# Where the norm weight goes: into the tokens' parts instead of every weight unit, low parts of weights on GpSimd, and the residual read back from memory

## The chip, the cores and the metric

The kernel runs on one core of one Trainium2 chip. The metric is the time of one execution on the device, in microseconds (us). TensorE (PE) multiplies matrices, PEld is its weight load; VectorE is DVE, ScalarE is ACT, GpSimd is POOL; SyncE (SP) issues most of the transfers between memory and the core's buffers.

## The reference

One inference step of two layers on 1032 tokens (1024 of a prompt, 8 decode tokens), 1024 features, float32. What matters here is where a norm stands ahead of a projection, and the residual:

```python
def rms_norm(x, w):
    y = x32 * lax.rsqrt(jnp.mean(x32 * x32, axis=-1, keepdims=True) + NORM_EPS)
    return (y * w.astype(jnp.float32)).astype(x.dtype)
...
    for layer in range(DEPTH):
        h = rms_norm(x, norm_mix[layer])
        ...                                   # layer 0: hybrid mixer, layer 1: SSD mixer; both begin with h @ w_in
        x = x + out                           # and end with @ w_out
        x = x + squared_relu_mlp(rms_norm(x, norm_mlp[layer]), mlp_w1[layer], mlp_w2[layer])
    return (rms_norm(x, norm_final), ...)
```

Layer 0 (gated delta rule and retention) projects 1024 features to 28 tiles of 128, layer 1 (SSD) to 40 and 32 columns more; each MLP goes to 4096 features and back.

## The kernel before

All activations lie with features on the partitions: a tile is 128 features by 1032 tokens. The residual stream x is held as two exact parts, `xh[k]` (rounded to float32r) and `xl[k]` (the rest), 8 tiles each. A weight is split in the same way, and a product is three matmuls (`mm3`, lines 150 to 152): high by high, high by low, low by high, each 128 x 128 by 344 tokens.

`load_w` (line 132) brings a weight unit [128, 512]: a transfer by SyncE into `raw` (3 buffers), then for a projection behind a norm GpSimd scales `raw` by the norm weights of its features (line 140), ScalarE copies it to the high part `whi` (line 144), and VectorE takes the low part `wlo` (line 145). The units of the second projections (`w_out`, `w2`), which have no norm weight, leave line 140 out and take their low part on GpSimd. The pairs of parts have 6 buffers, thus three units. The norm's other factor, the reciprocal root `rstd_bc`, scales the products when they leave the accumulators.

Stages, in order: the head (`load_x`: tokens arrive, `xh`, `xl`, their squares, the first tile's products); the hybrid mixers, where pieces of the projections are emitted between pieces of the mixers' chunk recurrences; near their end `out_first` (line 466), the first 3 (layer 1: 4) k-tiles of the output projection for all 8 m-tiles in three pieces of 344 tokens, to which the residual is added, before the sum goes to memory (`accd`); `out_proj` (line 1328), which loads these sums into `acc`, adds the remaining k-tiles and splits the new residual (`split_piece`, line 225); the MLP (`up`: a hidden tile, squared and split; `down`: a block of four hidden tiles onto `acc`); the same for layer 1 with the SSD mixer (`ssd_group`, line 1569). In `ssd_group` VectorE makes `xdt` (line 1600) and the masked scores `sc` (line 1613), and TensorE's decay products (line 1621) follow them.

In `out_first` the sum of a piece is built in `ost`: VectorE adds the product and `xh` (line 473), GpSimd adds `xl` (line 474), SyncE stores it (line 475). In layer 0 pieces 0 and 1 of an m-tile share a buffer of which there are two ("cs"), piece 2 has one buffer ("rb"); in layer 1 an m-tile's three pieces share one of four buffers.

Each engine works its instructions off in a fixed order. That order isn't the text's: a scheduler sets it when the program is built, so the change moves instructions beyond the edited lines. Each instruction waits for the semaphores of those it depends on.

Of the kernel before, what the change touches and what calls it, by code (L numbers as in the profile page):

```python
# [19 lines left out]
T = 1032                     # 1024 prompt tokens, then 8 decode tokens  # L20
# [24 lines left out]
# order of the hybrid projection's m-tiles (first column of each)  # L45
# [14 lines left out]
# blocks of the output projections: the first packed column's k-tile, the mixer outputs  # L60
# [13 lines left out]
# columns of the retention's constants  # L74
# [9 lines left out]
class Pools:  # L84
    """A mixer's two pools: what the output projection's first block needs or reuses, and the rest."""
# [10 lines left out]
class Kern:  # L96
    def __init__(self, ctx, tc, I, O):
# [20 lines left out]
        self.xl = [self.xp.tile([P, T], F32R, name=f"xl{k}") for k in range(KT)]  # L118

# [12 lines left out]
    def load_w(self, src, n, normw=None, lo_eng=None, dst=None, norm_eng=None):  # L132
        """src [128, n] of a packed weight unit -> exact float32r high and low parts."""
        nc = self.nc
        raw = self.wp.tile([P, 512], F32, tag="raw", name="raw", bufs=3)
        nc.sync.dma_start(raw[:, :n], src)
        if normw is not None:
            k = normw.shape[1]
            r3 = raw[:, :n].rearrange("p (k c) -> p k c", k=k)
            (norm_eng or nc.gpsimd).tensor_tensor(out=r3, in0=r3, in1=normw.unsqueeze(2).to_broadcast([P, k, n // k]), op=ALU.mult)  # L140
# [3 lines left out]
        nc.scalar.copy(hi[:, :n], raw[:, :n])  # L144
        (lo_eng or nc.vector).tensor_tensor(out=lo[:, :n], in0=raw[:, :n], in1=hi[:, :n].bitcast(F32), op=ALU.subtract)  # L145
        return hi, lo
# [7 lines left out]
    def load_half(self, src, kh, M, normw):  # L154
        return self.load_w(src[:, kh * 4 * M:(kh + 1) * 4 * M], 4 * M, normw[:, kh * 4:kh * 4 + 4])
# [9 lines left out]
    def products(self, src, M, normw, pss):  # L165
        """The products of an m-tile over the model dimension; yields after every sixth."""
        for kh in range(2):
            hi, lo = self.ahead.pop(0) if self.ahead else self.load_half(src, kh, M, normw)
# [12 lines left out]
    def gemm_units(self, src, M, normw, evict, other=False):  # L181
# [11 lines left out]
        for u, n in enumerate(self.products(src, M, normw, pss)):  # L193
# [31 lines left out]
    def split_piece(self, m, n, src, ssq, tp):  # L225
        """src [128, 344] fp32 becomes the residual's piece (m, n); its squares go to ssq."""
        nc = self.nc
        s = NSL[n]
        nc.scalar.copy(self.xh[m][:, s], src)  # L229
        nc.vector.tensor_tensor(out=self.xl[m][:, s], in0=src, in1=self.xh[m][:, s].bitcast(F32), op=ALU.subtract)  # L230
        self.square_piece(m, n, src, ssq, tp)
# [11 lines left out]
    def rsqrt(self, out, src):  # L243
        """out = (src) ** -0.5 for a small tile."""
# [7 lines left out]
    def rstd_from(self):  # L252
        """rstd_bc[:, t] = (sum_p ssq[p, t] / 1024 + eps) ** -0.5 on every partition; ssq lies where rstd_bc does."""
# [42 lines left out]
    def load_x(self, gp):  # L296
        """The tokens, as exact parts; their rstd; and the narrow projection, not yet scaled by it."""
# [15 lines left out]
        w0 = [self.load_half(I["wih"][0], 0, 128, normw)]  # L313
# [9 lines left out]
        def square(m):  # L323
            """x[m]'s squares; those of four tiles are added up."""
# [19 lines left out]
        for m in range(KT):  # L344
            nc.scalar.copy(self.xh[m], xr[m])
            nc.vector.tensor_tensor(out=self.xl[m], in0=xr[m], in1=self.xh[m].bitcast(F32), op=ALU.subtract)
# [4 lines left out]
            if m == 1:  # L351
                w0.append(self.load_half(I["wih"][0], 1, 128, normw))
# [21 lines left out]
    def softplus(self, out, x, tp, tag, bufs=None):  # L374
        """log1p(exp(x)) = max(x, 0) + 2 atanh(u / (2 + u)), u = exp(-|x|)."""
# [40 lines left out]
    def silu2(self, x, scale, tp):  # L416
        """x (1 + tanh(scale x)) in place, in two halves."""
# [6 lines left out]
    def layer(self, l):  # L424
        tc = self.tc
        nk = 16 if l else 8
        with ExitStack() as es:
            dp = es.enter_context(tc.tile_pool(name=f"spill{l}", bufs=1, space=bass.MemoryType.DRAM))
# [5 lines left out]
            with ExitStack() as es_op:  # L434
# [11 lines left out]
                self.out_proj(name, blocks, acc, tp, parts)  # L446
# [10 lines left out]
    def load_mixed(self, k, raw, hi, lo):  # L457
        """A spilled mixer output [128, 1024] and its decode columns, as exact parts."""
# [7 lines left out]
    def out_first(self, name, c0, parts, stage):  # L466
        """The first k-tiles of an output projection, with the residual, go to memory."""
        nc = self.nc

        def ev(m, n, ps):  # L470
            s = NSL[n]
            r = stage(n)
            nc.vector.tensor_tensor(out=r, in0=ps, in1=self.xh[m][:, s].bitcast(F32), op=ALU.add)
            nc.gpsimd.tensor_tensor(out=r, in0=r, in1=self.xl[m][:, s].bitcast(F32), op=ALU.add)
# [5 lines left out]
    def hyb_mixers(self, gp):  # L480
# [5 lines left out]
        def proj(dst, off=0):  # L486
            normw = self.V("mix0", 0, 8)
# [3 lines left out]
            yield from self.gemm_units(I["wih"][next(wi)], 128, normw, ev)  # L491
# [23 lines left out]
        def ret(t, rr, vv, gg):  # L515
            for i in range(2):
# [3 lines left out]
                for q in range(4):          # the halves of each head's features change places  # L520
# [25 lines left out]
        def step():  # L546
            """Emits a sixth of a projection (and the end of the one before)."""
# [6 lines left out]
        def project(n):  # L554
            """Emits the projections up to tile n."""
# [6 lines left out]
        def weave(mix, need, rate):  # L562
            """Emits a mixer's pieces with `rate` sixths of a projection after each."""
# [16 lines left out]
        # the output projection's first block fills in while the last mixers finish  # L580
# [22 lines left out]
    def gdn_setup(self, gp, ba):  # L603
# [14 lines left out]
        gnh = gp.tile([P, 5], F32, name="gnh")     # norm weights of the gated outputs, halved  # L618
# [4 lines left out]
        # beta and decay: [8, T] -> token-major [128, 9, 8]  # L623
# [35 lines left out]
        # rows of the cumulated decay, as exact float32r parts stacked on the contraction  # L659
# [19 lines left out]
    def gdn_head(self, gp, h, feat, st):  # L679
# [21 lines left out]
        for bi in range(2):  # L701
# [33 lines left out]
            # decay, transposed: DT[j, c, i] = exp(min(G_i - G_j, mask))  # L735
# [1150 lines left out]
```

## Time and profile before

| | |
|---|---|
| time, median of 3 runs | 3255.57 us |
| lowest and highest run | 3240.14 and 3257.78 us |
| profiled execution: first to last instruction | 3239.5 us |
| busy: TensorE, VectorE, ScalarE, GpSimd | 3086.4, 1740.3, 896.2, 1241.3 us |
| granted TensorE clock, mean | 0.960 |
| scaling of weight units (line 140) | 264 units, 300.7 us of GpSimd |
| low parts on VectorE (line 145) | 264 units, 209.6 us |
| low parts on GpSimd (line 145) | 179 units, 223.7 us |

The profile gives its span alone for the profiled execution, 3239.5 us; of the three runs the lowest, 3240.14 us, is 0.6 us longer than this span, and what lies around a span is not told otherwise. Rows read "line engine operation out<-in, shapes, xcount | busy us, mean ns of one | idle time of the engine before them, and what ended most of it". Rows of waits read "who <- whom: us in total, times, longest". A matmul's busy time overlaps its neighbours', so busy is not the same as at full rate; the granted clock says at which share of its full clock TensorE was let run.

### The profile page before, as it was taken

What the parts mean: (1) busy time and instruction counts of PE and PEld (TensorE: products, weight loads), DVE (VectorE), ACT (ScalarE), POOL (GpSimd) and SP (SyncE); (2) the same over time, 40 slices, a digit from 0 to 9 for tenths busy, and PEclk for the clock granted to TensorE, in tenths of its full rate; (3) what the DMA queues carried; (4) which work ended last, traced back from release to release, by engine and by line L of the source; (5) the groups of instructions that cost most, each with busy time, mean ns of one, the idle gap of its engine ahead of it and who ended that gap; (6) DMA issues with size and microseconds to landing.
All of it is one profiled execution on the core that took longest, in us unless ns stands there. A gap on an engine that the chain in (4) does not pass through costs nothing. (4 is left out here: it accounts for less than half of the span.)

```text
span 3239.5 us, 49390 instructions
## 1 busy us (share of the span) xinstructions
PE 3086.4 (95%) x19566; PEld 2929.6 (90%) x19566; DVE 1740.3 (54%) x3201; ACT 896.2 (28%) x1828; POOL 1241.3 (38%) x1234
## 2 busy tenths in 40 slices
PE   7989998989999999999999999999899999999998
PEld 6888888879999999999987788887899999999998
DVE  7664667464333333337886785967635333333334
ACT  3222221223111111114444444354213111111112
POOL 4232324155333323225355555444625332332324
PEclk9899999889999999999998898998899999999999
DMA  3011103142111111111111111222431111111112
GB/s 123 20 47 54 47 26 112 55 168 64 46 46 47 49 46 46 48 48 40 55 56 58 69 62 43 82 69 79 157 140 43 46 47 49 46 46 50 46 46 72
DMA packets 102326, 202.13 MB, mean 62 GB/s; under 512 B 12624, under 2 KB 27728, under 8 KB 102096
## 3 DMA queue, kind: packets, MB, share of 16 engines
q1 hardware_dynamic: 94800, 173.82, 16.7%
q0 software_dynamic: 7296, 25.17, 2.0%
q8 instruction: 154, 2.52, 0.3%
q14 instruction: 76, 0.62, 0.1%
HBM read 157.94 MB, written 38.89 MB: 61 GB/s over the span
## 5 line engine op out<-in xcount | busy, mean ns | idle before, releaser
L150 PE MATMUL pg<-xh,whi 128*128 128x344 f32 x3072 | 1020.7, 332 | 10.2 <-DVE sxc L1451 6.5
L152 PE MATMUL pg<-xh,wlo 128*128 128x344 f32 x3072 | 1012.9, 330 | 2.8 <-DVE wlo L145 2.8
L151 PE MATMUL pg<-xl,whi 128*128 128x344 f32 x3072 | 1009.0, 328 | 0.0
L150 PEld LDWEIGHTS pg<-xh,whi 128*128 128x128 f32 x3072 | 593.0, 193 | 27.7 <-issue 8.8
L152 PEld LDWEIGHTS pg<-xh,wlo 128*128 128x128 f32 x3072 | 592.8, 193 | 12.7 <-issue 5.2
L144 ACT CAST whi<-raw 128x512 fp32r<-128x512 f32 (+2 forms) x443 | 271.0, 612 | 1191.5 <-PE pg L151 723.9
L151 PEld LDWEIGHTS pg<-xl,whi 128*128 128x128 f32 x3072 | 592.3, 193 | 8.8 <-issue 5.8
L140 POOL TENSOR_TENSOR raw<-raw,vec 128x512 f32<-128x512 f32 x264 | 300.7, 1139 | 589.9 <-DMA raw<-w 339.7
L151 PE MATMUL pg<-alo,whi 128*128 128x344 f32 (+2 forms) x1476 | 472.4, 320 | 0.0
L152 PE MATMUL pg<-ahi,wlo 128*128 128x344 f32 (+2 forms) x1476 | 472.3, 320 | 0.0
L150 PE MATMUL pg<-ahi,whi 128*128 128x344 f32 (+2 forms) x1476 | 471.6, 319 | 0.0
L1236 DVE TENSOR_TENSOR acc<-acc,pg 128x344 f32<-128x344 f32 x360 | 182.8, 511 | 385.4 <-PE pg L152 385.4
L145 POOL TENSOR_TENSOR wlo<-raw,whi 128x512 fp32r<-128x512 f32 (+2 forms) x179 | 223.7, 1251 | 327.7 <-ACT whi L144 326.6
L145 DVE TENSOR_TENSOR wlo<-raw,whi 128x512 fp32r<-128x512 f32 x264 | 209.6, 794 | 193.3 <-ACT whi L144 172.2
L1227 POOL TENSOR_TENSOR r<-r 128x344 f32<-128x344 f32 x192 | 145.9, 760 | 387.6 <-ACT ahi L1226 338.5
L152 PEld LDWEIGHTS pg<-ahi,wlo 128*128 128x128 f32 x1476 | 277.6, 188 | 0.0
L150 PEld LDWEIGHTS pg<-ahi,whi 128*128 128x128 f32 x1476 | 277.5, 188 | 0.0
L151 PEld LDWEIGHTS pg<-alo,whi 128*128 128x128 f32 x1476 | 277.3, 188 | 0.0
L1228 DVE TENSOR_TENSOR alo<-r,ahi 128x344 fp32r<-128x344 f32 x192 | 135.6, 707 | 253.8 <-POOL r L1227 253.8
L1226 ACT ACTIVATE ahi<-r 128x344 fp32r<-128x344 f32 x192 | 94.5, 492 | 338.5 <-DVE r L1225 338.5
L1225 DVE SCALAR_TENSOR_TENSOR r<-pg,rstd_bc 128x344 f32<-128x344 f32 x186 | 94.8, 510 | 76.9 <-PE pg L152 75.6
L150 PE MATMUL pg<-mhi,whi 128*128 128x344 f32 x408 | 131.3, 322 | 4.1 <-DVE acc L1342 4.1
(534 smaller groups left out, 4422.9 us busy)
## 6 DMA issues: line engine op xcount, KB each, us to landing
raw<-w SPq DMA_DIRECT2D x256, 256.0 KB, 2.6
raw<-wis SPq DMA_DIRECT2D x80, 256.0 KB, 2.6
raw<-wih SPq DMA_DIRECT2D x56, 256.0 KB, 2.6
mraw<-spill SPq DMA_DIRECT2D x17, 512.0 KB, 4.1
accd<-ost SPq DMA_DIRECT2D x48, 172.0 KB, 2.1
acc<-accd SPq DMA_DIRECT2D x16, 516.0 KB, 6.9
dS<-sstate SPq DMA_DIRECT2D x32, 256.0 KB, 3.5
o_sssm<-dS POOLq DMA_DIRECT2D x32, 256.0 KB, 2.4
```

What stands on the lines that cost most here:

```text
L140: (norm_eng or nc.gpsimd).tensor_tensor(out=r3, in0=r3, in1=normw.unsqueeze(2).to_broadcast([P, k, n // k]), op=ALU.mult)
L144: nc.scalar.copy(hi[:, :n], raw[:, :n])
L145: (lo_eng or nc.vector).tensor_tensor(out=lo[:, :n], in0=raw[:, :n], in1=hi[:, :n].bitcast(F32), op=ALU.subtract)
L150: t.matmul(ps, lhsT=whi, rhs=xhi, start=start, stop=False)
L151: t.matmul(ps, lhsT=whi, rhs=xlo, start=False, stop=False)
L152: t.matmul(ps, lhsT=wlo, rhs=xhi, start=False, stop=stop)
L1225: nc.vector.scalar_tensor_tensor(out=r, in0=ps, scalar=0.0, in1=self.rstd_bc[:, s], op0=ALU.max, op1=ALU.mult)
L1226: nc.scalar.activation(hi[:, s], r, AF.Square)
L1227: nc.gpsimd.tensor_tensor(out=r, in0=r, in1=r, op=ALU.mult)
L1228: nc.vector.tensor_tensor(out=lo[:, s], in0=r, in1=hi[:, s].bitcast(F32), op=ALU.subtract)
L1236: nc.vector.tensor_tensor(out=s, in0=s, in1=ps, op=ALU.add)
```

## The change

1. Norm weights: `load_w` no longer scales. Where the residual is split, both parts carry the norm weights of the norm that follows: ScalarE's copy becomes a copy with a scale for each partition, VectorE's subtraction becomes (x * w) - high. The sums of squares still take the unscaled x. The narrow projection of the head, which reads the tokens themselves, keeps its scaled weights.
2. Low parts: all of them are now taken on GpSimd.
3. Residual: as the parts no longer hold x itself, `out_first` loads each piece of x from memory into `ost` and adds the product on top. In layer 0 it comes from the input, in layer 1 from `resd`, which the last block of layer 0's MLP fills by transfers that GpSimd issues.

```diff
     def __init__(self, ctx, tc, I, O):
...
+        rp = ctx.enter_context(tc.tile_pool(name="resd", bufs=1, space=bass.MemoryType.DRAM))
+        self.resd = [rp.tile([P, T], F32, name=f"resd_{m}") for m in range(KT)]
...
-    def load_w(self, src, n, normw=None, lo_eng=None, dst=None, norm_eng=None):
+    def load_w(self, src, n, lo_eng=None, dst=None):
         raw = self.wp.tile([P, 512], F32, tag="raw", name="raw", bufs=3)
         nc.sync.dma_start(raw[:, :n], src)
-        if normw is not None:
-            k = normw.shape[1]
-            r3 = raw[:, :n].rearrange("p (k c) -> p k c", k=k)
-            (norm_eng or nc.gpsimd).tensor_tensor(out=r3, in0=r3, in1=normw.unsqueeze(2).to_broadcast([P, k, n // k]), op=ALU.mult)
...
         nc.scalar.copy(hi[:, :n], raw[:, :n])
-        (lo_eng or nc.vector).tensor_tensor(out=lo[:, :n], in0=raw[:, :n], in1=hi[:, :n].bitcast(F32), op=ALU.subtract)
+        (lo_eng or nc.gpsimd).tensor_tensor(out=lo[:, :n], in0=raw[:, :n], in1=hi[:, :n].bitcast(F32), op=ALU.subtract)
...
-    def split_piece(self, m, n, src, ssq, tp):
-        s = NSL[n]
-        nc.scalar.copy(self.xh[m][:, s], src)
-        nc.vector.tensor_tensor(out=self.xl[m][:, s], in0=src, in1=self.xh[m][:, s].bitcast(F32), op=ALU.subtract)
+    def split(self, m, s, src, w):
+        nc.scalar.activation(self.xh[m][:, s], src, AF.Copy, scale=w)
+        nc.vector.scalar_tensor_tensor(out=self.xl[m][:, s], in0=src, scalar=w, in1=self.xh[m][:, s].bitcast(F32), op0=ALU.mult, op1=ALU.subtract)
+
+    def split_piece(self, m, n, src, ssq, tp, norm):
+        self.split(m, NSL[n], src, self.V(norm, m))
         self.square_piece(m, n, src, ssq, tp)
...
     def load_x(self, gp):
-            nc.scalar.copy(self.xh[m], xr[m])
-            nc.vector.tensor_tensor(out=self.xl[m], in0=xr[m], in1=self.xh[m].bitcast(F32), op=ALU.subtract)
+            self.split(m, slice(0, T), xr[m], self.V("mix0", m))
...
     def layer(self, l):
+            if l == 0:
+                self.resid = lambda m: self.I["xT"][:, m, :]
+            else:
+                self.resid = lambda m: self.resd[m]
...
     def out_first(self, name, c0, parts, stage):
             r = stage(n)
-            nc.vector.tensor_tensor(out=r, in0=ps, in1=self.xh[m][:, s].bitcast(F32), op=ALU.add)
-            nc.gpsimd.tensor_tensor(out=r, in0=r, in1=self.xl[m][:, s].bitcast(F32), op=ALU.add)
+            nc.sync.dma_start(r, self.resid(m)[:, s])
+            nc.vector.tensor_tensor(out=r, in0=r, in1=ps, op=ALU.add)
             nc.sync.dma_start(self.accd[m][:, s], r)
...
     def down(b):                              # in mlp
                     if b == HID // 4 - 1:
-                        self.split_piece(m, n, s, ssq, tp)
+                        self.split_piece(m, n, s, ssq, tp, "mix1")
+                        if n == 2:
+                            nc.gpsimd.dma_start(self.resd[m], acc[m])
...
     def ssm_setup(self, gp):
-                nc.gpsimd.tensor_tensor(out=raw, in0=raw, in1=normw[:, k:k + 4].unsqueeze(2).to_broadcast([P, 4, 32]), op=ALU.mult)
```

The rest of the diff hands the norm's name on to `split_piece` and takes the argument `normw` out of the calls. The counts of instructions by engine: TensorE the same, VectorE 264 fewer, GpSimd 42 fewer (266 scalings and 48 additions out, 264 low parts and 8 issues in), SyncE 48 more.

What stands where. On VectorE, in the third step of the first group of the SSM mixers (`sxc` is a projection leaving the accumulators, `x` the convolution, `dS` and `dy` the decode states), before:

```order
L421 SCALAR_TENSOR_TENSOR x<-th,x 128x516
L1727 SCALAR_TENSOR_TENSOR dS<-dbc,dxd,dS 128x128 x3
L421 SCALAR_TENSOR_TENSOR x<-th,x 128x516
L1451 TENSOR_TENSOR sxc<-pg,rstd_bc 128x344
L145 TENSOR_TENSOR wlo<-raw,whi 128x512
L1731 TENSOR_REDUCE dy<-dpr 128x4
L1451 TENSOR_TENSOR sxc<-pg,rstd_bc 128x344 x2
L1600 TENSOR_TENSOR xdt<-pm,dt 128x512
```

and now, in the same place (line numbers behind the edits have moved by one or two):

```order
L1726 SCALAR_TENSOR_TENSOR dS<-dbc,dxd,dS 128x128 x3
L421 SCALAR_TENSOR_TENSOR x<-th,x 128x516
L1450 TENSOR_TENSOR sxc<-pg,rstd_bc 128x344
L421 SCALAR_TENSOR_TENSOR x<-th,x 128x516
L1730 TENSOR_REDUCE dy<-dpr 128x4
L1450 TENSOR_TENSOR sxc<-pg,rstd_bc 128x344 x2
L1599 TENSOR_TENSOR xdt<-pm,dt 128x512
```

The low part has gone from between the two `sxc`, and half of a convolution's gate (L421) stands there instead.

On SyncE, at the end of layer 0's first block (`accd` the stored sums, `woh` weights, `mraw` a mixer's output for the next block), before:

```order
L475 DMA accd_6_103<-ost 128x344
L475 DMA accd_7_104<-ost 128x344 x2
L136 DMA raw<-woh 128x256
L475 DMA accd_7_104<-ost 128x344
L1335 DMA acc_0_6973<-accd_0_97 128x1032
```

and now:

```order
L479 DMA accd_6_113<-ost 128x344
L479 DMA accd_7_114<-ost 128x344
L477 DMA ost<-xT 128x344
L479 DMA accd_7_114<-ost 128x344
L138 DMA raw<-woh 128x256
L479 DMA accd_6_113<-ost 128x344
L477 DMA ost<-xT 128x344
L479 DMA accd_7_114<-ost 128x344
L138 DMA raw<-woh 128x384
L1338 DMA acc_0_6927<-accd_0_107 128x1032
```

The loads of the residual stand between the stores, each ahead of the store of the piece that it begins, and weights and the reload of `acc` stand behind them.

More of the change, by code (lines that the diff above doesn't have):

```diff
@@ L152, in mm3, with load_half @@
         t.matmul(ps, lhsT=wlo, rhs=xhi, start=False, stop=stop)
-    def load_half(self, src, kh, M, normw):
-        return self.load_w(src[:, kh * 4 * M:(kh + 1) * 4 * M], 4 * M, normw[:, kh * 4:kh * 4 + 4])
+    def load_half(self, src, kh, M):
+        return self.load_w(src[:, kh * 4 * M:(kh + 1) * 4 * M], 4 * M)
     def narrow(self, ps, w, x, k):
@@ L163, in narrow, with products @@
             self.nc.tensor.matmul(ps[32 * n:32 * n + M, 0:c.stop - c.start], lhsT=w, rhs=x[:, c], start=k == 0, stop=k == KT - 1)
-    def products(self, src, M, normw, pss):
+    def products(self, src, M, pss):
         for kh in range(2):
-            hi, lo = self.ahead.pop(0) if self.ahead else self.load_half(src, kh, M, normw)
+            hi, lo = self.ahead.pop(0) if self.ahead else self.load_half(src, kh, M)
             for n in range(3):
@@ L179, in others, with gemm_units @@
         return [self.pm(), self.ps2(), self.ps2()]
-    def gemm_units(self, src, M, normw, evict, other=False):
+    def gemm_units(self, src, M, evict, other=False):
         if self.first:
@@ L192, in gemm_units @@
         pss = self.others() if other else [self.pg() for n in range(3)]
-        for u, n in enumerate(self.products(src, M, normw, pss)):
+        for u, n in enumerate(self.products(src, M, pss)):
             if u == 0:
@@ L214, in gemm_flush @@
                 k1 = min(kn, k0 + cut)
-                hi, lo = self.load_w(src(m)[:, k0 * 128:k1 * 128], (k1 - k0) * 128, None, self.nc.gpsimd)
+                hi, lo = self.load_w(src(m)[:, k0 * 128:k1 * 128], (k1 - k0) * 128)
                 w += [(hi[:, i:i + 128], lo[:, i:i + 128]) for i in range(0, (k1 - k0) * 128, 128)]
@@ L312, in load_x @@
         fetch(1)
-        w0 = [self.load_half(I["wih"][0], 0, 128, normw)]
+        w0 = [self.load_half(I["wih"][0], 0, 128)]
         nc.vector.tensor_scalar(out=self.ones_r, in0=self.ident, scalar1=0.0, scalar2=1.0, op0=ALU.mult, op1=ALU.add)
@@ L351, in load_x @@
             if m == 1:
-                w0.append(self.load_half(I["wih"][0], 1, 128, normw))
+                w0.append(self.load_half(I["wih"][0], 1, 128))
             if m > 1:
@@ L445, in layer @@
                 acc = [ap.tile([P, T], F32, name=f"acc{l}_{m}") for m in range(KT)]
-                self.out_proj(name, blocks, acc, tp, parts)
+                self.out_proj(name, blocks, acc, tp, parts, "mlp%d" % l)
             self.mlp(l, acc, l == 1)
@@ L486, in proj @@
         def proj(dst, off=0):
-            normw = self.V("mix0", 0, 8)
             def ev(n, ps):
                 nc.vector.tensor_tensor(out=dst[:, off + n * NW:off + (n + 1) * NW], in0=ps, in1=self.rstd_bc[:, NSL[n]], op=ALU.mult)
-            yield from self.gemm_units(I["wih"][next(wi)], 128, normw, ev)
+            yield from self.gemm_units(I["wih"][next(wi)], 128, ev)
         def gate(k, zs):
@@ L1228, in ev @@
                     nc.vector.tensor_tensor(out=lo[:, s], in0=r, in1=hi[:, s].bitcast(F32), op=ALU.subtract)
-                self.gemm_tile(I["w1"][l, t], 128, normw, ev, t == 1)
+                self.gemm_tile(I["w1"][l, t], 128, ev, t == 1)
             def down(b):
@@ L1249, in finish @@
                         dst = (w[:, 0:512], w[:, 512:1024])
-                    ws.append(self.load_w(I["w2"][l, b, m], 512, None, nc.gpsimd, dst))
+                    ws.append(self.load_w(I["w2"][l, b, m], 512, nc.gpsimd, dst))
                 def norm(s0, s1, sqs):
@@ L1325, in mlp, with out_proj @@
                 self.rstd = self.rstd_from()
-    def out_proj(self, name, blocks, acc, tp, parts):
+    def out_proj(self, name, blocks, acc, tp, parts, norm):
         nc, tc = self.nc, self.tc
@@ L1343, in ev @@
                     if last:
-                        self.split_piece(m, n, o, ssq, tp)
+                        self.split_piece(m, n, o, ssq, tp, norm)
                 for _ in self.gemm_flush(lambda m: self.I[name][m, :, c0 * 128:c0 * 128 + w], cur, ev):
@@ L1380, in ssm_setup @@
         self.first = self.others()
-        for u, _ in enumerate(self.products(I["wis"][4], 128, normw, self.first)):
+        for u, _ in enumerate(self.products(I["wis"][4], 128, self.first)):
             if u == 1:
@@ L1443, in ssm_mixers @@
         st = self.ssm_setup(gp)
-        normw = self.V("mix1", 0, 8)
         def conv_tile(dst, ti, gst, gco):
@@ L1451, in ev @@
                 nc.vector.tensor_tensor(out=xc[:, 3 + n * NW:3 + (n + 1) * NW], in0=ps, in1=self.rstd_bc[:, NSL[n]], op=ALU.mult)
-            self.gemm_tile(I["wis"][ti // 4 * 10 + ti % 4 if ti < 16 else ti % 4 * 10 + ti // 4], 128, normw, ev)
+            self.gemm_tile(I["wis"][ti // 4 * 10 + ti % 4 if ti < 16 else ti % 4 * 10 + ti // 4], 128, ev)
             nc.gpsimd.tensor_scalar(out=gco, in0=xc[:, 3 + 1021:3 + 1032], scalar1=1.0, scalar2=None, op0=ALU.mult)
@@ L1476, in ev @@
                 nc.vector.scalar_tensor_tensor(out=z[:, NSL[n]], in0=ps, scalar=0.5, in1=self.rstd_bc[:, NSL[n]], op0=ALU.mult, op1=ALU.mult)
-            self.gemm_tile(I["wis"][g * 10 + 6 + i], 128, normw, ev)
+            self.gemm_tile(I["wis"][g * 10 + 6 + i], 128, ev)
             self.silu2(z, 1.0, gp)
```

2 lines of the change are left out of this document (removed).

## The prediction

> **What bounds the kernel now.** I read the busy line and the clock line of the page first, then the stages cut out of the span, then who ended TensorE's waits in the stages where it waits at all.
>
> ```profile
> PE 3086.4 (95%) x19566; PEld 2929.6 (90%) x19566; DVE 1740.3 (54%) x3201; ACT 896.2 (28%) x1828; POOL 1241.3 (38%) x1234
> ```
>
> By stage (columns: stretch, its length, each engine's busy time with its instructions, granted clock, DMA share, GB/s):
>
> ```profile
> core 0: us, PE busy (x) PEld busy (x) DVE busy (x) ACT busy (x) POOL busy (x), PEclk, DMA share, GB/s
> 0.00:82.00 82.00, 63.59 (x369) 51.90 (x370) 64.35 (x105) 30.55 (x51) 35.73 (x37) 0.92 0.37 121
> 82.00:648.00 566.00, 521.66 (x3672) 473.15 (x3671) 353.49 (x856) 139.36 (x292) 169.48 (x212) 0.94 0.16 52
> 648.00:718.00 70.00, 62.34 (x340) 53.09 (x340) 43.87 (x89) 12.94 (x21) 40.33 (x41) 0.87 0.40 140
> 810.00:1455.00 645.00, 645.00 (x4102) 645.00 (x4101) 222.44 (x398) 113.30 (x201) 197.77 (x199) 1.00 0.15 47
> ...
> 1530.00:2260.00 730.00, 683.03 (x4099) 605.74 (x4098) 560.39 (x887) 330.88 (x755) 350.58 (x313) 0.92 0.18 62
> 2260.00:2350.00 90.00, 76.49 (x434) 73.09 (x433) 62.59 (x92) 20.91 (x27) 58.75 (x49) 0.91 0.44 157
> ```
>
> The MLP of layer 0 (810 to 1455) is TensorE without a gap at clock 1.00; the MLP of layer 1 is its copy. Nothing done on VectorE or GpSimd can shorten those two, some 1290 us. The time to win lies in the head (TensorE idle 18.4 of 82 us), the hybrid mixers (44.3 of 566), the SSM mixers (47.0 of 730) and the two stretches in which the output projection's first block fills in (7.7 of 70, 13.5 of 90), and in their clocks below 1.00.
>
> Who ended the waits, first in 1530 to 2260, then in 82 to 648, then the head and the two first blocks (us in total, times, longest):
>
> ```profile
> PE pm L1621 <- DVE xdt L1600: 14.0, 8, 3.0
> PE pm L1621 <- DVE sc L1613: 13.0, 5, 3.4
> ...
> PE pg L152 <- DVE wlo L145: 2.6, 3, 1.7
> ...
> PE ps L906 <- DVE Y L902: 10.0, 8, 2.3
> PE pm L730 <- DVE tokq L723: 4.3, 5, 1.9
> ...
> PE pm L337 <- DVE sqx L330: 5.3, 1, 5.3
> PE pg L150 <- DVE ost L473: 4.9, 2, 2.8
> ```
>
> Nearly all are VectorE's. So the question is what stands in VectorE's queue ahead of those releasers. One wait, in order of time (start, length, instruction; in brackets the idle time before it):
>
> ```profile
> 1674.53 1.30 POOL L1730 TENSOR_TENSOR dpr<-dS,dbc 128x512 f32<-128x512 f32 x1
> 1674.58 1.80 DVE L145 TENSOR_TENSOR wlo<-raw,whi 128x512 fp32r<-128x512 f32 x1
> ...
> 1677.75 0.67 DVE L1600 TENSOR_TENSOR xdt<-pm,dt 128x512 f32<-128x512 f32 x1
> 1678.48 0.50 PE L1621 MATMUL pm<-sgrow,ssel 64*128 64x256 f32 x2 [1.98 <-DVE xdt L1600]
> ```
>
> A weight's low part, 1.80 us long beside a GpSimd operation, stands three instructions ahead of `xdt`, and TensorE waits 1.98 us. The clock before, in and after that wait:
>
> ```profile
> 1668.00:1676.00 8.00, 8.00 (x56) 7.99 (x55) 8.00 (x12) 2.51 (x4) 4.94 (x6) 1.00 0.16 66
> 1676.40:1678.50 2.10, 0.12 (x2) 0.03 (x1) 2.10 (x5) 0.64 (x1) 0.25 (x1) 1.00 0.38 123
> 1679.80:1686.40 6.60, 6.60 (x21) 5.12 (x20) 6.21 (x8) 4.08 (x16) 2.83 (x3) 0.50 0.00 0
> ```
>
> After it the clock is 0.50 for 6.6 us: a wait costs itself and some of the microseconds behind it.
>
> **The change part by part.**
>
> ```profile
> L140 POOL TENSOR_TENSOR raw<-raw,vec 128x512 f32<-128x512 f32 x264 | 300.7, 1139 | 589.9 <-DMA raw<-w 339.7 <-DMA raw<-wis 104.5 <-DMA raw<-wih 76.9
> ...
> L145 DVE TENSOR_TENSOR wlo<-raw,whi 128x512 fp32r<-128x512 f32 x264 | 209.6, 794 | 193.3 <-ACT whi L144 172.2 <-PE pg L152 12.3 <-DMA rf<-xr 2.4
> L145 POOL TENSOR_TENSOR wlo<-raw,whi 128x512 fp32r<-128x512 f32 x155 | 201.1, 1298 | 296.4 <-ACT whi L144 295.3 <-POOL ost L474 0.9
> ...
> L474 POOL TENSOR_TENSOR ost<-ost,xl 128x344 f32<-128x344 f32 x48 | 49.6, 1046 | 25.9 <-DVE ost L473 23.3 <-issue 1.6 <-PE pm L1043 0.9
> ...
> L145 DVE TENSOR_TENSOR wlo<-raw,whi 128x512 fp32r<-128x512 f32 x73 | 73.2, 1002 | 12.9 <-PE pg L152 11.8 <-ACT whi L144 0.9
> L145 DVE TENSOR_TENSOR wlo<-raw,whi 128x512 fp32r<-128x512 f32 x47 | 33.2, 707 | 9.8 <-ACT whi L144 5.9 <-DMA rf<-xr 2.4 <-ACT X L801 0.8
> ```
>
> (The last two are the same instruction in 1530 to 2260 and in 82 to 648.)
>
> GpSimd loses 264 x 1.139 = 301 us of scaling and 50 us of L474, and gains 264 x 1.298 = 343 us of low parts: a load about as before. VectorE loses 210 us. The way of a weight from landing to use loses one operation (scale, high, low becomes high, low).
>
> *SSM mixers.* VectorE gives up 73.2 of 560.4 us, in pieces of 1.0 us. The eight `xdt` waits are 1.75 us each; a wlo ahead is worth 1.0 (the mean) to 1.8 us (the row above), so I take 9 of their 14 us; the 2.6 us for wlo itself turn into a wait for GpSimd's wlo, which comes one operation sooner, and I take 2; of `sc` and the rest I take 2. That is 13 us of idle time. Clock 0.92 over 730 us is 58 us of lost clock against 47.0 us of idle, 1.2 for one; I count 0.9, since part of it falls where other engines bound: 12 us. Together -25; bounds 0 (another operand ends each wait) and -73.2 (VectorE's queue alone sets the stage).
>
> A rule against such a price: the Trainium skill, "TensorE: Matmul & The Clock Gate", section "HAM oscillation", warns of idle gaps above about 3.4 us. By it the 1.98 us wait would cost no clock, the clock terms here and below would be nought and the sum -22 in place of -35; the trace shows 0.50 right after that shorter wait, so I keep the row.
>
> *Hybrid mixers.* 33.2 of 353.5 us leave VectorE, in pieces of 0.7. The `tokq` waits are 0.9 us each with a wlo at most in front; of them and of `Y` I take 4 us of idle and 3 of clock (0.94 over 566 us is 34 us, against 44.3 idle: 0.77). -7; bounds 0 and -33.2.
>
> *Head.* The sum for the first norm (`sqx`, L330) runs on VectorE behind two low parts, and TensorE waits 5.3 us for it; half of that goes, -3. Scaling while splitting needs the norm weights before the first copy: they land before the narrow projection's weights, which TensorE waits for anyway. Bounds -5.3 and +2.
>
> *Splitting with a scale.* VectorE's two forms cost the same (first pair), ScalarE's scaled form may cost more (second pair: 510 ns for 256 columns against 481 for 344).
>
> ```profile
> L1451 DVE TENSOR_TENSOR sxc<-pg,rstd_bc 128x344 f32<-128x344 f32 x69 | 34.4, 508 | 17.5 <-PE pg L152 17.1
> L1476 DVE SCALAR_TENSOR_TENSOR z<-pg,rstd_bc 128x344 f32<-128x344 f32 x48 | 24.0, 508 | 18.9 <-PE pg L152 18.9
> ...
> L1640 ACT ACTIVATE x<-x,vec 128x256 f32<-128x256 f32 x64 | 29.3, 510 | 27.5 <-PE pm L1598 27.4
> L229 ACT CAST xh<-acc 128x344 fp32r<-128x344 f32 x72 | 34.6, 481 | 63.1 <-DVE acc L1342 45.1 <-DVE acc L1236 17.3
> ```
>
> At 0.15 us more each, 72 pieces give 11 us, spread over three stretches in which ScalarE is free more than half of the time: 0. If that cover were gone, +4 at each end of a sum of squares.
>
> *The residual from memory, layer 0's first block.* L474 leaves (24 x 1.05 us of GpSimd). In its place each of the 24 pieces is loaded by SyncE, which issues in order and has the stores and weights in the same queue. A piece's buffer must see its store land, then its load, before VectorE may add:
>
> ```profile
> accd<-ost SPq DMA_DIRECT2D x48, 172.0 KB, 2.1
> ...
> 701.79 0.52 DVE L473 TENSOR_TENSOR ost<-pg,xh 128x344 f32<-128x344 f32 x1 [2.83 <-DMA accd<-ost]
> ...
> SPq L475 <- POOL ost L474: 45.8, 23, 10.8
> ```
>
> The third piece has one buffer ("rb"): 2.1 store + 2.1 load + 0.5 add, with issues about 5.5 us a round, against 70/8 = 8.8 us for one m-tile. It is hidden on the mean, but not in the hurried last tiles, where a landing store already holds VectorE up (2.83 us). I count two rounds of 2.5 us of delay and 2 us of clock, less 3 for L474: +4. Bounds -8 and +20 (all eight tiles held 2.5 us).
>
> *Layer 1's first block* has four whole-tile buffers, so the loads run ahead; the waits for `ost` (4.9 us) lose the 24 GpSimd additions behind them: -5, bounds -13 and +10.
>
> *Saving the residual.* Eight issues on GpSimd at the end of layer 0, 0.58 us each by L1728's mean:
>
> ```profile
> L1728 POOL DMA_DIRECT2D o_sssm<-dS x32 | 18.6, 580 | 23.0 <-DVE dS L1727 21.4 <-DVE bc L409 1.2 <-DVE sc L1613 0.4
> ```
>
> They stand between the additions of the squares and the low parts there; +1, bounds 0 and +4.6.
>
> *The two MLPs and later blocks.* 0: 128 of the 264 scalings go and 128 low parts come on a GpSimd that is busy 198 of 645 us; VectorE's release helps nobody, as TensorE has no gap. The next thing late would be a low part behind three squarings, 1.3 us against the three weight buffers ahead.
>
> Sum: -25 -7 -3 +4 -5 +1 = -35 us. The profiled execution's span of 3239.5 is within 0.6 us of the lowest of the three runs (3240.1); their median is 15.4 us higher. 3240.1 - 35 = 3205; I cannot tell which kind of run will be the changed kernel's median, so I add half the difference: **3212 us**, faster by 1.3% than the median. The forecast's own range is 3170 to 3239.
>
> **The rivals.**
>
> *The waits stay.* VectorE's freed time becomes idle time, because the releasers (`sc`, `Y`) also wait for ScalarE and TensorE; `sc`, with 13.0 us the second on the list, speaks for it. Moved work then yields the head and the blocks alone, -4 to +10 and the scatter of the runs: 3250. The Trainium skill, "Perfetto Trace Analysis", section "Optimizing Scalar/DVE Operations", says that offloading between VectorE and GpSimd might not help as they share a port; the 1.80 us wlo beside `dpr` agrees that they hinder each other, but scaling already ran on GpSimd, so its load hardly grows here.
>
> *Slower: SyncE's queue holds the weights.* 48 loads more, each behind the landing of a store; what is queued behind a held load are weight units and the reload of the accumulators. For it: SyncE already stood 45.8 us for `ost` there. If each of the 16 m-tiles of the two blocks costs 2.1 + 2.1 us with as much clock again for half of them, that is 67 + 33 = 100 us, less 35 won elsewhere: 3256 + 65 = about 3320; with layer 0's block alone about 3285. It decides once a round takes longer than 8.8 us there. Against it: four buffers in layer 1, five pieces in layer 0.
>
> *VectorE bounds the SSM stage outright.* Then most of the 73.2 and 33.2 us come off, and their clock: 3240 - 90 = 3150, with the scatter 3158.
>
> **How the numbers follow.** Forecast 0.64, waits stay 0.17, queue 0.13, VectorE bound 0.06. What a measurement can tell from no change is about 0.5%, 16 us. The forecast and the last rival are faster, but the forecast's tail over 3239 (0.02) counts as same; of "waits stay" all is the same but 0.01, which is slower. Faster 0.68, same 0.18, slower 0.14. The range 3155 to 3275 leaves out the queue (0.13) and half of the last (0.03) and a little of the others.
>
> **What would show it.** In the SSM mixers VectorE's busy time falls by some 70 us with GpSimd's within 15 us; the waits of L1621 for `xdt` go from 14.0 to about 5 us; the clock there rises from 0.92 to 0.94 or more; the stage shortens by about 25 us. In layer 0's first block VectorE's additions wait for loads of `ost`. The MLPs stay at 645 us. I am wrong if the waits for `xdt` stay, if TensorE begins to wait for GpSimd's low parts, or if the 70 us stretch grows beyond 90.

## The result, and the profile after

The changed kernel is slower: 3273.95 us median (3265.93 to 3284.09, 17 runs) against 3256.08 us (3238.43 to 3269.09, 17 runs), a ratio of 1.0060 with a 95% interval of 1.0046 to 1.0074, or about 20 us. I had forecast 3212. The profiled execution spans 3269.0 us. Its busy line:

```profile
PE 3106.4 (95%) x19566; PEld 2944.2 (90%) x19566; DVE 1585.7 (49%) x2937; ACT 906.8 (28%) x1828; POOL 1244.0 (38%) x1192
```

VectorE is 155 us less busy, not 210. Both kernels issue 19566 matmuls, so the stages can be cut at the same counts of them. Hybrid mixers, layer 0's first block with the start of its output projection, SSM mixers, layer 1's first block, first of the kernel before:

```profile
86.90:638.00 551.10, 510.17 (x3603) 462.38 (x3602) 344.98 (x842) 134.82 (x286) 167.38 (x209) 0.94 0.16 49
638.00:787.70 149.70, 135.86 (x801) 124.88 (x800) 84.39 (x160) 44.09 (x92) 83.07 (x84) 0.93 0.38 131
1543.70:2257.90 714.20, 667.66 (x4002) 590.74 (x4001) 544.62 (x857) 326.67 (x748) 346.88 (x308) 0.91 0.18 63
2257.90:2411.20 153.30, 136.40 (x801) 132.39 (x802) 89.50 (x139) 33.07 (x43) 73.27 (x61) 0.93 0.45 159
```

and of the changed one (columns as in the prediction's table by stage):

```profile
89.90:659.20 569.30, 523.90 (x3601) 472.25 (x3601) 331.45 (x794) 134.98 (x285) 171.12 (x209) 0.92 0.16 49
659.20:820.50 161.30, 141.41 (x801) 130.60 (x801) 78.01 (x156) 46.47 (x92) 54.20 (x57) 0.87 0.44 142
1575.90:2293.30 717.40, 671.36 (x4003) 591.18 (x4002) 507.59 (x789) 328.60 (x747) 357.10 (x309) 0.91 0.19 64
2293.30:2442.70 149.40, 133.84 (x803) 130.99 (x802) 80.08 (x136) 32.93 (x43) 49.36 (x37) 0.94 0.57 187
```

The hybrid mixers are 18 us longer, layer 0's first block 12, the SSM mixers 3, layer 1's first block is 4 shorter. These are single executions, and a stage's length holds its clock: a run below (e3), in which neither the hybrid mixers' work nor TensorE's order there was changed, took 569.3 us for them in its profiled execution too, with TensorE idle for 40.7 us against 40.9 before. In the changed kernel TensorE is idle for 45.4 us there, for 46.0 in the SSM mixers (46.5 before), and for 19.9 in layer 0's first block (13.8). VectorE gave up 33.2 us of low parts in the hybrid mixers and about 73 in the SSM mixers, yet is only 13.5 and 37.0 us less busy: half came back as longer instructions. The waits of TensorE, in the hybrid mixers, the SSM mixers and layer 0's first block:

```profile
PE ps L908 <- DVE Y L904: 9.4, 8, 1.9
PE pm L710 <- DVE fv L421: 7.8, 2, 4.0
PE pm L772 <- DVE lr L770: 5.6, 3, 2.0
...
PE pm L1620 <- DVE sc L1612: 14.3, 5, 3.9
PE pm L1620 <- DVE xdt L1599: 13.9, 9, 4.0
...
PE pg L148 <- DVE ost L478: 7.0, 2, 4.4
PE pg L148 <- DVE acc L1345: 4.2, 1, 4.2
```

The waits for `xdt` have not moved (14.0 before), and two that hardly stood in the list of before are new: `fv` (0.7) and `lr` (1.8). One of the waits for `lr`, in order of time:

```profile
111.55 0.23 DVE L766 TENSOR_TENSOR lc<-lc,lh 128x64 f32<-128x64 f32 x1
111.58 1.31 POOL L143 TENSOR_TENSOR wlo<-raw,whi 128x512 fp32r<-128x512 f32 x1 [1.51 <-ACT whi L142]
111.69 1.75 DVE L770 TENSOR_TENSOR lr<-lh,c 128x512 fp32r<-128x512 f32 x1
...
113.37 0.68 DVE L770 TENSOR_TENSOR lr<-lc,c 128x512 fp32r<-128x512 f32 x1
113.59 0.47 PE L772 MATMUL pm<-lr,blk 128*128 128x512 f32 x1 [1.81 <-DVE lr L770]
```

This is the loss in one picture. VectorE's first `lr` begins 0.11 us after GpSimd's low part and takes 1.75 us; the second, alike but with GpSimd idle, takes 0.68. It ends 0.55 us after GpSimd's instruction does: for most of the time until then it stood still. The low part has left VectorE's queue and holds VectorE up from GpSimd's. The Trainium skill, "SBUF — State Buffer", section "SBUF: two separate sides", says that the two engines share one pair of ports as an exclusive lock, held for a whole instruction, which a VectorE instruction with two operands in the core's memory needs while GpSimd reads there; this row agrees.

Summed over the whole trace, TensorE's matmuls wait 136.6 us for VectorE, 123.0 before. For parts of weights they wait 0.2 us, 6.6 before, and the weight loads 3.6 us, 11.7 before. So TensorE doesn't stand waiting for low parts that come late.

### The profile page after: what moved, and what is told of

Same layout as the page of the kernel before. It is cut to its first block, busy times and chain, and to the rows that moved or that the text cites. A ratio compares the mean times of both kernels' runs of the same rounds, so it can differ in the third digit from the quotient of the medians.

```text
span 3269.0 us, 48877 instructions
## 1 busy us (share of the span) xinstructions
PE 3106.4 (95%) x19566; PEld 2944.2 (90%) x19566; DVE 1585.7 (49%) x2937; ACT 906.8 (28%) x1828; POOL 1244.0 (38%) x1192
## 5 line engine op out<-in xcount | busy, mean ns | idle before, releaser
L143 POOL TENSOR_TENSOR wlo<-raw,whi 128x512 fp32r<-128x512 f32 (+2 forms) x443 | 580.9, 1312 | 1167.3 <-ACT whi L142 1091.1
L149 PE MATMUL pg<-mlo,whi 128*128 128x344 f32 x408 | 132.3, 324 | 0.0
L150 PE MATMUL pg<-mhi,wlo 128*128 128x344 f32 x408 | 132.2, 324 | 0.0
```

The costliest lines, as they stand in the source:

```text
L143: (lo_eng or nc.gpsimd).tensor_tensor(out=lo[:, :n], in0=raw[:, :n], in1=hi[:, :n].bitcast(F32), op=ALU.subtract)
L149: t.matmul(ps, lhsT=whi, rhs=xlo, start=False, stop=False)
L150: t.matmul(ps, lhsT=wlo, rhs=xhi, start=False, stop=stop)
```

## The experiments

**Which part of the change costs?** The change is three edits that can be had apart. e1 is the changed kernel with

```diff
-        return self.load_w(src[:, kh * 4 * M:(kh + 1) * 4 * M], 4 * M)
+        return self.load_w(src[:, kh * 4 * M:(kh + 1) * 4 * M], 4 * M, self.nc.vector)
```

> The changed kernel, but the low parts of the projections' weight units are taken on VectorE again, as before (the second projections' stay on GpSimd). Norm weights in the split and residual from memory stay. Theory A (GpSimd's low parts cost: VectorE's short steps of the recurrences wait for them, 1.75 us in place of 0.68): this kernel keeps the gain of the scaling that left GpSimd and loses the cost; 3230 to 3250 us, faster than the kernel before, other VectorE work as long as before or shorter, hybrid mixers not longer than before. Theory B (the residual from memory costs: loads of ost in SyncE's queue): it stays as slow as the changed kernel, 3265 to 3280.

e2 is the kernel before with

```diff
-        (lo_eng or nc.vector).tensor_tensor(out=lo[:, :n], in0=raw[:, :n], in1=hi[:, :n].bitcast(F32), op=ALU.subtract)
+        (lo_eng or nc.gpsimd).tensor_tensor(out=lo[:, :n], in0=raw[:, :n], in1=hi[:, :n].bitcast(F32), op=ALU.subtract)
```

> The kernel before with one edit: all low parts on GpSimd (scaling of the units stays there too, residual unchanged). Theory A: slower than before, 3265 to 3300, with the waits of L708 for fv and L770 for lr and a longer hybrid stage; GpSimd is then busier than in the changed kernel by the 301 us of scaling, so it may be slower still than that one. Theory B: within 8 us of the kernel before.

e3 is the kernel before with

```diff
...
-            nc.vector.tensor_tensor(out=r, in0=ps, in1=self.xh[m][:, s].bitcast(F32), op=ALU.add)
-            nc.gpsimd.tensor_tensor(out=r, in0=r, in1=self.xl[m][:, s].bitcast(F32), op=ALU.add)
+            nc.sync.dma_start(r, self.resid(m)[:, s])
+            nc.vector.tensor_tensor(out=r, in0=r, in1=ps, op=ALU.add)
...
+                            nc.gpsimd.dma_start(self.resd[m], acc[m])
```

> The kernel before with one edit: out_first loads each piece of the residual from memory and GpSimd saves the residual at the end of layer 0. Theory A: layer 0's first block and the start of the output projection 8 to 12 us longer, the rest as before: 3256 to 3268. Theory B: all of the loss, 3268 to 3280.

e4 is the changed kernel with

```diff
-            nc.sync.dma_start(r, self.resid(m)[:, s])
+            nc.scalar.dma_start(r, self.resid(m)[:, s])
```

> The changed kernel, but the 48 loads of the residual are issued by ScalarE's queue in place of SyncE's. Theory A: at most the 8 to 12 us of layer 0's first block can come off: 3262 to 3275. Theory B: the weights no longer stand behind the loads, most of the loss goes: 3250 to 3260.

| kernel | median us | ratio to before (95%) | at full clock | lost to the clock |
|---|---|---|---|---|
| before (39 runs beside these) | 3253 to 3257 | 1 | 3110.8 | 142.8 |
| changed | 3273.95 | 1.0060 (1.0046 to 1.0074) | 3123.7 | 150.2 |
| e1 low parts on VectorE | 3210.05 | 0.9858 (0.9833 to 0.9884) | 3088.2 | 119.3 |
| e2 only low parts on GpSimd | 3335.55 | 1.0240 (1.0213 to 1.0266) | 3147.8 | 184.1 |
| e3 only the residual | 3268.62 | 1.0038 (1.0017 to 1.0058) | 3121.0 | 144.2 |
| e4 loads by ScalarE | 3273.76 | 1.0059 (1.0038 to 1.0080) | 3122.3 | 150.6 |

The last two columns are means over the runs: span x granted clock, called the time at full clock, and the rest of the span. The former scatters by 4.3 us (standard deviation) over the 39 runs of before, the latter by 9.5, so most of what differs between two executions of one kernel is clock.

The directions are theory A's, and theory B falls with e1 and e2: the loss goes with the low parts. A's sizes were off, though. e1 came out 20 us below A's range (3230 to 3250) and e2 36 us above it (3265 to 3300); e3's median lies 0.6 us past A's range, at the edge of B's. The residual from memory costs 0.4% (e3), taking the norm weights out of the units gains 1.8% (0.9858 against 1.0038, e3 to e1), and the low parts on GpSimd cost 2.0% (0.9858 to 1.0060, e1 to the change): +12 - 59 + 66 us, the last two to about 10 us each, which makes the +20. With the scaling still on GpSimd the same move costs 2.4% (e2). e4 agrees with the change within the 0.2% of its interval: there is no sign that SyncE's order of issue is where the residual costs. e1's hybrid and SSM mixers (the counts of matmuls as above):

```profile
80.00:629.00 549.00, 517.49 (x3598) 469.82 (x3597) 336.06 (x841) 134.21 (x285) 117.72 (x165) 0.92 0.17 51
1545.00:2233.00 688.00, 650.29 (x4003) 576.80 (x4003) 516.50 (x857) 325.75 (x748) 262.23 (x236) 0.94 0.20 66
```

and its low parts on VectorE in these two stretches, from the groups of instructions (columns as in the prediction's groups):

```profile
L143 DVE TENSOR_TENSOR wlo<-raw,whi 128x512 fp32r<-128x512 f32 x46 | 33.2, 721 | 12.2 <-ACT whi L142 10.6 <-ACT X L803 0.9 <-PE pg L150 0.5
L143 DVE TENSOR_TENSOR wlo<-raw,whi 128x512 fp32r<-128x512 f32 x73 | 64.8, 887 | 14.6 <-PE pg L150 11.8 <-ACT whi L142 2.7
```

VectorE's other work here is 336.1 - 33.2 = 302.9 us and 516.5 - 64.8 = 451.7; in the changed kernel, which has nothing else there, it is 331.5 and 507.6. GpSimd's low parts thus cost VectorE 29 and 56 us in longer instructions, 84 us, to spare it 98.

The scaling had such a price too, a smaller one. In e3, which still has it, VectorE's other work in these two stretches is 346.4 - 33.0 = 313.4 and 549.0 - 72.2 = 476.8 us, 11 and 25 above e1's, and its low parts took 7 us more than in e1. One of them in the kernel before:

```profile
1777.69 1.04 POOL L140 TENSOR_TENSOR raw<-raw,vec 128x512 f32<-128x512 f32 x1 [1.48 <-DMA raw<-wis]
1777.83 1.45 DVE L145 TENSOR_TENSOR wlo<-raw,whi 128x512 fp32r<-128x512 f32 x1
```

With GpSimd idle it takes 0.69 us; here it ends 0.55 us after GpSimd's scaling, as `lr` did after the low part. From e3 to e1 TensorE's waits for VectorE fall from 133.4 to 110.2 us, those for parts of weights from 5.5 to 1.3: the shorter way of a weight is the smaller part of the gain.

**Is it the hold-up, or that low parts come later, or the moved order?** In e2 and in the change the order of the matmuls moves too: place by place, 2870 and 2842 of the 19566 in the traces differ from the kernel before, 237 in e1. e6 is e1 with one more GpSimd instruction for each unit, whose result nothing reads; 557 places differ from e1:

```diff
...
+            nc.gpsimd.tensor_tensor(out=raw[:, :n], in0=raw[:, :n], in1=hi[:, :n].bitcast(F32), op=ALU.subtract)
...
```

> e1 (norm weights in the split, low parts of the projections on VectorE) with one redundant instruction for each of the 264 units: after VectorE's low part GpSimd subtracts the high part from raw in place, and nothing reads the result. TensorE's order is that of e1 but for 203 of 18168 instructions, and no product waits for GpSimd. Theory A1 (VectorE's steps are held up while a GpSimd instruction with two operands runs): the loss comes back without any product waiting for it, 3250 to 3280 us, with VectorE's steps of 0.68 us again partly 1.2 to 1.8 us long. Theory A2 (the loss of low parts on GpSimd comes from the moved order, or from products that get their low part later): within 10 us of e1's 3210.

3289.91 us (3266.9 to 3297.21), ratio 1.0104 (1.0077 to 1.0130): 2.5% above e1, 10 us past the range of A1. TensorE's matmuls wait 2.5 us in all for parts of weights and never for a redundant instruction (two weight loads do, 1.5 us together); for VectorE they wait 143.8 us, against 110.2 in e1. One wait of its SSM mixers:

```profile
1815.12 1.30 POOL L1732 TENSOR_TENSOR dpr<-dS,dbc 128x512 f32<-128x512 f32 x1
1815.35 3.40 DVE L1489 TENSOR_TENSOR z<-z 128x1032 f32<-128x1032 f32 x1
1816.37 1.28 POOL L146 TENSOR_TENSOR raw<-raw,whi 128x512 f32<-128x512 f32 x1
1818.67 0.67 DVE L1733 TENSOR_REDUCE dy<-dpr 128x4 f32<-128x512 f32 x1
...
1822.59 0.68 DVE L1602 TENSOR_TENSOR xdt<-pm,dt 128x512 f32<-128x512 f32 x1
...
1823.32 0.58 PE L1623 MATMUL pm<-sgrow,ssel 64*128 64x256 f32 x1 [5.43 <-DVE xdt L1602]
```

`z` adds two tiles of that name, which takes 1.23 us alone. It stood behind two GpSimd instructions in a row, of which the redundant one is the second, until that one ended at 1817.65, and took 3.40 us. `xdt` reads the accumulators, has its own 0.68, and is late all the same, because of what stands ahead of it. So the hold-up without moved low parts costs at least as much as they do (80 us against 66). How much of the change's 66 us its moved order adds or takes off, no run tells apart.

e9 lets GpSimd fill `raw` with zeros in that place:

```diff
-            nc.gpsimd.tensor_tensor(out=raw[:, :n], in0=raw[:, :n], in1=hi[:, :n].bitcast(F32), op=ALU.subtract)
+            nc.gpsimd.memset(raw[:, :n], 0.0)
```

> As the redundant subtraction, but GpSimd fills raw with zeros instead: it writes and reads nothing from the core's memory. If it is the reading of operands that holds VectorE up, this stays within 8 us of e1's 3210, with VectorE's steps as in e1; if any GpSimd instruction does, it is slower in the measure of its GpSimd time, by 15 us or more where an instruction takes over 0.4 us.

3225.39 us (3216.59 to 3233.48), ratio 0.9913 (0.9883 to 0.9943): 0.55% above e1. By the medians that is 15.3 us, past the 8 us of the first half of the expectation and just at the 15 of the second; the traces speak for the first half all the same. The redundant instructions in e6's groups:

```profile
L146 POOL TENSOR_TENSOR raw<-raw,whi 128x512 f32<-128x512 f32 x264 | 352.9, 1337 | 563.5 <-DVE wlo L144 489.9 <-issue 51.8 <-ACT V L716 4.5
```

and in e9's:

```profile
L146 POOL MEMSET raw<- 128x512 f32 x264 | 138.9, 526 | 631.1 <-DVE wlo L144 365.2 <-issue 241.3 <-DVE xt L782 7.7
```

The SSM mixers of e6:

```profile
1584.20:2299.40 715.20, 661.80 (x4002) 584.91 (x4001) 550.54 (x858) 325.89 (x748) 362.42 (x309) 0.92 0.19 63
```

and of e9:

```profile
1561.40:2255.90 694.50, 655.32 (x4002) 581.08 (x4001) 518.54 (x857) 326.13 (x748) 298.24 (x309) 0.93 0.19 65
```

Against e1's 516.5 us VectorE is busy 34 us longer beside the subtractions and 2 beside the fills; in the measure of their GpSimd time the fills would cost it 13. The MLPs show it most plainly, where VectorE takes the low parts `alo` of the hidden tiles, first in e6, then in e9:

```profile
L1232 DVE TENSOR_TENSOR alo<-r,ahi 128x344 fp32r<-128x344 f32 x192 | 154.3, 805 | 252.8 <-POOL r L1231 252.8
L1232 DVE TENSOR_TENSOR alo<-r,ahi 128x344 fp32r<-128x344 f32 x192 | 120.1, 626 | 252.8 <-POOL r L1231 252.8
```

In both kernels 32 of them begin beside a redundant instruction: these take 1.59 us on the mean beside the subtraction and 0.52 beside the fill, and 0.52 is what they take with GpSimd idle. At full clock e9 is 4.5 us above e1 (3092.7), e6 45.3 (3133.5); the rest of e9's 15 us is clock, by which single runs of a kernel differ by 9 to 10 us. So an instruction of GpSimd that only writes hardly holds VectorE up; a small cost of the fills is left unexplained. Both kinds of redundant instruction keep `raw` from its next transfer, so e9 also speaks against that as the cause of e6's loss.

**Can the residual come back for less?** In e7, which is e1 otherwise, layer 0's first block no longer waits for loads:

```diff
     def ev(m, n, ps):                          # out_first
-            nc.sync.dma_start(r, self.resid(m)[:, s])
-            nc.vector.tensor_tensor(out=r, in0=r, in1=ps, op=ALU.add)
+            if name == "woh":
+                nc.scalar.copy(r, ps)
...
     def ev(m, n, ps):                          # out_proj; acc[m] is loaded with x, fst[m] with accd[m]
                     nc.vector.tensor_tensor(out=o, in0=o, in1=ps, op=ALU.add)
+                    if name == "woh":
+                        nc.vector.tensor_tensor(out=o, in0=o, in1=fst[m][:, NSL[n]], op=ALU.add)
...
```

> e1, and in layer 0 the residual no longer goes through out_first: ScalarE copies the products to ost, which are stored as before; out_proj loads x straight into acc (nothing to wait for) and adds the stored sum from three landing buffers while the last block's products leave the accumulators, 24 more VectorE additions there. Theory: the waits for ost (9.9 us) and acc (4.4 us) of layer 0's first block and output projection go, and a third to a half of the clock lost there (15.7 us): that stretch 161 to 145-150 us, the whole 3193 to 3202. Rival: the waits move on to the landing of the stored sums, or to VectorE's additional additions: 3205 to 3215.

3202.80 us (3196.32 to 3214.38), ratio 0.9846 (0.9819 to 0.9873): between the two ranges, 0.8 us past the theory's. The stretch of the block:

```profile
631.50:784.90 153.40, 137.20 (x802) 125.29 (x801) 86.04 (x160) 55.38 (x116) 51.25 (x53) 0.92 0.46 155
```

and TensorE's longest wait in it:

```profile
PE pg L149 <- ACT whi L143: 5.8, 1, 5.8
```

It went from 160.5 to 153.4 us, not to 145 to 150: the waits for `ost` and `acc` are gone, and one for a weight unit of 5.8 us took the place of two fifths of them. Beside e1 the whole gains 0.1%, which these runs can't tell from nothing.

**Does it go on?** The 16 maskings of the SSM mixers that run on GpSimd (`E<-E,sc`, 2.65 us each there, 1.33 on VectorE) go to VectorE in e8, with 32 scalings more (`xd`) in e10:

```diff
-                (gs if j else v).tensor_tensor(out=E[j], in0=E[j], in1=sc[:, j, :]...
+                v.tensor_tensor(out=E[j], in0=E[j], in1=sc[:, j, :]...
...
-                gs.tensor_tensor(out=v64(x2), in0=v64(xd), ...          # e10 alone
+                v.tensor_tensor(out=v64(x2), in0=v64(xd), ...
```

> e7, and in the SSM mixers all 32 maskings of the decays (E times sc, 128x1024) run on VectorE; 16 of them ran on GpSimd. GpSimd loses 16 x 2.65 = 42 us there, VectorE gains 16 x 1.33 = 21 us. Theory A1 (a GpSimd instruction with two operands holds VectorE up): VectorE's steps get less late than the addition costs, the SSM stage 5 to 10 us shorter, 3193 to 3200 us. Rival (VectorE's own queue bounds that stage): 5 to 20 us longer, 3208 to 3223.

> As the run with all maskings on VectorE, and the 32 scalings of xd (128x512) on VectorE too: GpSimd loses another 41 us, VectorE gains another 22. Here TensorE's order moves as well (1680 instructions). Theory A1: another 3 to 8 us off, 3188 to 3198. Rival (VectorE's queue bounds): slower than that run by 5 to 20 us.

e8: 3206.23 us, ratio 0.9839 (0.9814 to 0.9864); e10: 3202.01, 0.9829 (0.9806 to 0.9852). Both medians lie between the ranges of A1 and of the rival (e10's rival would be 3211 to 3226), so A1's sizes are missed twice. By ratio both are a little faster than e7, by no more than the intervals hide. The SSM mixers take 685.5 us in e7, 684.4 in e8 and 681.7 in e10, at full clock 644.4, 645.1 and 647.5. The instructions moved take VectorE 17.5 us in e8 and 43.7 in e10, yet it is only 5.5 and 16.0 us busier there: the rest came back in shorter instructions, which is A1's mechanism without a gain in time. The 5 to 20 us of the rival, by which VectorE's own queue bounds the stage, don't show either. e1, e7, e8 and e10 all beat both kernels; e10 is the fastest by ratio, 1.7% below before and 2.3% below the changed kernel (0.9829 against 1.0060).

## Why the prediction was wrong

*The step that failed* is the first line of the sum: "GpSimd loses 301 us of scaling and 50 us of L474, and gains 343 us of low parts: a load about as before. VectorE loses 210 us." I weighed GpSimd's load as time in its own queue. What the 264 units cost there is what they do to VectorE, for the scaling as for the low part. So I set the removal of the scaling at nothing, where it gives 59 us (e3 to e1), and the move of the low parts at a gain, where it costs 66. I had the row: the `wlo` of 1.80 us beside `dpr`. I read it as a price of VectorE's low part; it is the price of a GpSimd instruction. That the hold-up exists and is enough for the loss is shown (e6 against e9); how the 59 us divide between the hold-up and the shorter way of a weight was not run apart.

*The signs.* VectorE's busy time in the SSM mixers fell by 37 us, not 70, and the clock there stayed at 0.91. The waits for `xdt` stayed at 13.9 us, which I had named as a sign that I am wrong. The two other such signs didn't appear: TensorE's matmuls don't wait for GpSimd's low parts, and the stretch of 70 us takes 73.7 by the same matmuls.

*SSM mixers, -25.* They changed by +3.2 us (714.2 to 717.4); with the low parts left on VectorE (e1) they take 688.0.

*Hybrid mixers, -7.* They changed by +18.2 in this pair of executions. TensorE's idle time there rose by 4.5 us, the sum of its waits with those too short for the list; most of the rest is clock, which scatters (e3 has as much of it with no more idle time). e1 brings the idle time from 40.9 to 31.5 us.

*Head, -3.* It is 3 us longer (86.9 to 89.9 up to the 400th matmul), though the wait for `sqx` fell from 5.3 to 4.3 us; in e1 it ends at 79.4. Scaled splitting does no harm there that shows.

*Splitting with a scale, 0.* My pair of rows for VectorE reads the accumulators, and the split doesn't: with GpSimd idle `xl` takes 0.58 us where it took 0.52, and ScalarE's `xh` 0.58 on the mean where it took 0.48. No run has this by itself.

*Layer 0's first block, +4.* It changed by +11.6, inside the bounds of -8 and +20, and by +12.5 in e3. The mechanism was the one named, at more than twice the size: VectorE's additions wait for the landing of loads, as VectorE's own waits in this stretch of the changed kernel show,

```profile
DVE ost L478 <- DMA ost<-xT: 12.1, 4, 6.3
...
DVE acc L1345 <- DMA acc<-accd: 7.2, 1, 7.2
```

TensorE waits 7.0 us for the additions in `ost`, and then 4.2 us for one that waits for the stored sums. The queue, in which I saw the danger, shows no part in it (e4).

*Layer 1's first block, -5.* It changed by -3.9. *Saving the residual, +1.* No run has it by itself. *The MLPs, 0.* The MLP of layer 0 takes 629.4 or 629.5 us from the 4800th to the 8800th matmul in all eleven profiled kernels, whatever GpSimd does beside it.

*The rivals.* "The waits stay" was right in that the waits for `xdt` stayed, but the reason, that `sc` and `Y` wait for ScalarE and TensorE, was not the one, and its time was 24 us too low. The sentence of the Trainium skill, "Perfetto Trace Analysis", section "Optimizing Scalar/DVE Operations", on the shared port, which I set aside there because GpSimd's load hardly grows, was the rule to price: the load was there before too, and had its cost. Of the slower rival, SyncE's queue, there is no sign; its 3285 for layer 0's block alone doesn't come out of its own terms, which give 3256 + 50 - 35 = 3271.

*The base.* I summed from an execution that had lost 129 us to the clock, where the mean is 142.8. The term for the scatter, half of 15.4, made up for about half of these 13.7 us; the rest would have brought the forecast to some 3219.

*The clock.* "A wait costs itself and some of the microseconds behind it" held, at 0.9 us lost to the clock for each idle one between matmuls (129.1 to 143.8) in the profiled execution of before, but it goes by a grid, below.

## What to carry to other kernels

Before work is moved between VectorE and GpSimd, look in the trace for one VectorE instruction with two lengths, 0.68 and 1.75 us here: where the long one lies beside a GpSimd instruction that reads two tensors, that instruction is paid for on VectorE. Here such instructions taken off GpSimd altogether were a gain although GpSimd was only 38% busy (the scaling), those put there were a loss (the low parts), and those moved from it to VectorE made no difference that the runs can tell (e8, e10); in a stage where TensorE never waits all of it was free. Undo the parts of a change one by one: here two effects of some 60 us each nearly cancelled, and a kernel 1.4% faster than before was inside the slower one.

## What the runs showed of the hardware

*The clock goes by a grid.* The stretches at clock 0.50 all begin on one grid of 3.413 us in each execution, and all but the last of an execution are whole multiples of it long (of 349 stretches in eleven profiled kernels: 119 of one step, 65 of two, 70 of three, 95 longer). The wait of 3.96 us for `fv` in the changed kernel, cut at the grid:

```profile
392.94:396.35 3.41, 2.25 (x15) 1.97 (x13) 3.29 (x4) 0.73 (x2) 1.33 (x2) 1.00 0.08 11
396.35:399.77 3.42, 0.62 (x6) 0.65 (x7) 2.42 (x4) 1.16 (x2) 2.03 (x3) 1.00 0.19 65
399.77:403.18 3.41, 3.41 (x15) 2.64 (x13) 1.90 (x6) 1.76 (x3) 0.24 (x1) 0.50 0.00 0
403.18:406.60 3.42, 3.42 (x18) 3.42 (x17) 1.90 (x6) 0.63 (x1) 1.16 (x1) 0.50 0.04 7
406.60:410.01 3.41, 3.41 (x26) 3.39 (x25) 2.37 (x4) 0.66 (x2) 0.00 (x0) 1.00 0.00 0
```

Of the wait 1.16 us fall into the first step, which is followed by one at full clock, and 2.80 us into the second, which is followed by two at 0.50.

Of the steps at full clock, by TensorE's idle time in them, over the eleven profiled kernels:

| idle in the step, us | steps | followed by clock 0.50 |
|---|---|---|
| under 0.8 | 8899 | 68 |
| 0.8 to 1.2 | 254 | 14 |
| 1.2 to 1.6 | 121 | 21 |
| 1.6 to 2.0 | 91 | 63 |
| 2.0 and more | 183 | 178 |

Idle time beyond about half of one step is as a rule followed by half the clock in the next one. A wait of 2 us may fall into one step or be shared by two, which may be one way in which executions of one program, the kernel before, come to lose 126 to 163 us to the clock; that wasn't tested. The Trainium skill, "TensorE: Matmul & The Clock Gate", section "What's actually happening", has the free-running window of 3413 ns, and the grid agrees; the gap of about 3.4 us of its section "HAM oscillation", by which I said that the clock terms would be nought, is too long a limit for these traces, and the measurement decides.

*Which instructions are held up.* VectorE instructions that read the accumulators, such as `xdt<-pm,dt` (679 to 681 ns in the means of e1, e6 and the change), keep their length beside GpSimd; those that read two tensors of the core's memory, such as `lr<-lh,c` and `z<-z`, don't. Nor does a small copy within that memory, `rh<-rs`: it takes 0.17 us (the median in the kernel before) and 1.01 us where it starts beside a scaling.
